# x, B, C and twelve gate blocks as seven block products at the front, staged in DRAM, with the state-space chunks beside the heads

## Chip, core and metric

The kernel runs on one core of a Trainium2 chip. The metric is device time in microseconds (us) for one launch, on that core. TensorE (PE) multiplies, VectorE (DVE), ScalarE (ACT) and GpSimd (POOL) do the elementwise work, and SyncE (SP) issues nearly all DMAs, in one queue and in the order of the program.

## What is computed

One decoder layer with two causal token mixers side by side, 1024 tokens by 1024 channels, all in float32:

```
h = RMSNorm(x)
[q|k|v|z_a | xBC | z_s | dt | gates] = h @ w_in        # 4096 + 3072 + 2048 + 32 + 2048 columns
attention: 8 heads, two softmax maps each, a = p0 - lam*p1, RMS-normed, times silu(z_a)  -> y_a
state space: xBC = silu(conv4(xBC)); 32 heads in 4 groups, 8 chunks of 128 tokens a group;
             group RMSNorm(y * silu(z_s))                                                -> y_s
merged = sigmoid(g_a)*(y_a @ w_proj_attn) + sigmoid(g_s)*(y_s @ w_proj_ssd)
out = x + merged @ w_out
```

Float32 products are kept accurate by splitting each operand into a high and a low part in the fp32r format: high·high + high·low + low·high, three matmuls for each product. The split is a ScalarE copy (high) and a subtraction on VectorE or GpSimd (low).

## The kernel before

The normalised h lies transposed in SBUF as two tiles, hH and hL (8 row blocks of 128 channels by 1024 tokens). Four kinds of projection run over it, all in matmuls of 512 output columns, and this order is the bulk of TensorE's program (`bulk`): head 0, dt, heads 1 to 7 (`att_proj`, PSUM tile pma), z of group 0 (pmz), then per group x, B and C (`ssd_proj_xbc`, pc) and z, then sixteen gate blocks (`gates`, pg). An attention head's scores, softmax, transposes and value product (`att_core`, `att_block`: sc, p, pa, av, pya) run beside the projections of the following heads. A group's eight chunks (`ssd_core`, `ssd_chunk`: px, pb, pO, pS, pD, py, and the decay tile ab) run beside the projections of the next group, and the last group's beside the gates. x, B and C go through a depthwise convolution of four taps (`conv`: three VectorE passes of nearly 1024 columns, then tanh on ScalarE and one more pass) and stay in SBUF as tiles cv, as z stays in tiles zs.

At the end come three products (`products(c)`: the two halves of y_s, then y_a, against their weights) and the output projection (`final`, po). These three products already go by a scheme with seven block multiplications for a 2 x 2 by 2 x 2 block product, where the plain one has eight. Its sums of the left operand, t1 to t4, are made on GpSimd and staged in DRAM (`prepare`, `sums_of`, t_d), read back and split into forms (`fill`), its sums of weights are made in `pair_splits`, and its seven products go into three PSUM banks X, Y and Z that are recombined in `pair_step`:

```
ORDER = (("b11", 1), ("t2", 6), ("b21", 2), ("t3", 7), ("t1", 5), ("t4", 4), ("b22", 3))
BEFORE = {2: "ct", 7: ("u", 6), 4: ("u", 7), 3: "c22"}
into = {1: x, 6: y, 2: x, 7: y, 5: z, 4: y, 3: z}
```

BEFORE names what must have been read out of a bank before the product of that number may go into it.

The order of every engine's program is fixed when the kernel is built, by a planner in the kernel itself (`Plan`). Each stage is a generator that emits instructions and yields the time at which it wants to go on. Costs are formulas in the helpers; on VectorE an op of n columns is put down as 0.07 + 0.00104 n us (`tt`, `stt`), whatever it meets on the chip. The bulk generator runs whenever no task is due. Buffers are counted in Slots: 19 large SBUF tiles (bigs), 12 of 2 KB a partition (mids), 4 raw weight tiles, 9 split weight tiles, and PSUM in three rings: mm 2 banks, sc 2 tiles of 2 banks, tr 2 banks. `PACE` is the planned time between chunk starts, 13 us. On the chip the engines keep that order and wait on semaphores.

In the profile most instructions carry a helper's line: L167 is every matmul, L176 every transpose, L191 every ScalarE activation, L196 two-tensor ops of VectorE and GpSimd, L201 VectorE's scalar-tensor-tensor ops, L213 every DMA, L647 the masked score copy. So the groups are told apart by tile names.

## Time and profile before

| | |
|---|---|
| median of 3 runs | 1678.44 us (1678.04 to 1679.87) |
| profiled execution | 1677.29 us, span 1675.5 us, granted clock 0.998 |
| TensorE, VectorE, ScalarE, GpSimd busy | 1638.2, 1084.8, 815.9, 530.5 us |
| matmul records | 8226 |
| DMA | 194.47 MB, mean 116 GB/s |
| heads (first matmul to last) | 11.0 to 563.8 us |
| x, B, C (pc) | 626.2 to 1065.7 us |
| gates (pg) | 1122.5 to 1338.3 us |
| three products | 1338.5 to 1583 us |

A row of a group reads: line, engine, operation, what it writes <- reads, shape, xcount | total busy us, mean ns of one | idle time of the engine before them and what ended it. A row of a table by stage reads: stretch, its length, then for each engine busy us and instruction count, then TensorE's granted clock, the DMA engines' busy share and GB/s. A row of waits reads: who waited for whom, total us, times, longest us.

### The profile page before, as it was taken

What the parts mean: (1) busy time and instruction counts of PE and PEld (TensorE: products, weight loads), DVE (VectorE), ACT (ScalarE), POOL (GpSimd) and SP (SyncE); (2) the same over time, 40 slices, a digit from 0 to 9 for tenths busy, and PEclk for the clock granted to TensorE, in tenths of its full rate; (3) what the DMA queues carried; (4) which work ended last, traced back from release to release, by engine and by line L of the source; (5) the groups of instructions that cost most, each with busy time, mean ns of one, the idle gap of its engine ahead of it and who ended that gap; (6) DMA issues with size and microseconds to landing.
All of it is one profiled execution on the core that took longest, in us unless ns stands there. A gap on an engine that the chain in (4) does not pass through costs nothing.

```text
span 1675.5 us, 23517 instructions
## 1 busy us (share of the span) xinstructions
PE 1638.2 (98%) x8226; PEld 1364.6 (81%) x8226; DVE 1084.8 (65%) x1902; ACT 815.9 (49%) x1971; POOL 530.5 (32%) x616
## 2 busy tenths in 40 slices
PE   7999999999999999999999999999999999989999
PEld 5788888888888888888888888888778887767887
DVE  6686676666765744589578658846654167878821
ACT  5646566565665542466365455535534245233410
POOL 4323233231341210132243233236764433333100
PEclk9999999999999999999999999999999999999999
DMA  6202021120210202322142133227769657787832
GB/s 191 55 19 64 7 58 34 31 63 7 57 51 14 63 29 69 87 88 64 50 133 83 39 101 107 57 81 245 257 214 334 211 167 264 238 289 244 290 120 69
DMA packets 168740, 194.47 MB, mean 116 GB/s; under 512 B 11557, under 2 KB 114734, under 8 KB 168622
## 3 DMA queue, kind: packets, MB, share of 16 engines
q1 hardware_dynamic: 168622, 192.97, 35.9%
q8 instruction: 65, 1.06, 0.3%
q14 instruction: 53, 0.43, 0.1%
HBM read 143.51 MB, written 49.41 MB: 115 GB/s over the span
## 4 chain that ended last, share of the span: by engine, by line
PE 82%; DVE 5%; POOL 4%; issue 4%; ACT 3%; DMA 2%; SPq 0%; POOLq 0%; DVEq 0%; ACTq 0%
PE pma L167 17%; PE pc L167 15%; PE pmz L167 9%; PE pg L167 7%; PE po L167 5%; PE pY L167 4%; PE sc L167 4%; PE av L167 4%; PE pX L167 3%; PE pD L167 3%; PE pZ L167 2%; PE pa L176 2%; POOL ts L196 1%; ACT qh L191 1%; PE pS L167 1%
## 5 line engine op out<-in xcount | busy, mean ns | idle before, releaser
L167 PE MATMUL pma<-w,hH 128*128 128x512 f32 x1024 | 343.0, 405 | 0.1
L167 PE MATMUL pc<-hH,w 128*128 128x512 f32 x768 | 243.5, 394 | 0.0
L167 PEld LDWEIGHTS pma<-w,hH 128*128 128x128 f32 x1024 | 189.2, 190 | 34.6 <-ACT hH L191 0.5
L167 PE MATMUL pma<-w,hL 128*128 128x512 f32 x512 | 206.4, 403 | 0.0
L191 ACT ACTIVATE w<-raw 128x512 fp32r<-128x512 f32 (+1 forms) x194 | 120.4, 625 | 126.8 <-PE pc L167 45.7
L196 POOL TENSOR_TENSOR w<-raw,w 128x512 fp32r<-128x512 f32 (+1 forms) x62 | 83.2, 1342 | 265.1 <-ACT w L191 259.2
L167 PEld LDWEIGHTS pc<-hH,w 128*128 128x128 f32 x768 | 142.9, 188 | 28.1
L167 PE MATMUL pmz<-w,hH 128*128 128x512 f32 x512 | 165.4, 397 | 0.0
L167 PE MATMUL pg<-hH,w 128*128 128x512 f32 x512 | 161.9, 393 | 0.0
L196 DVE TENSOR_TENSOR w<-raw,w 128x512 fp32r<-128x512 f32 x132 | 111.1, 848 | 66.5 <-ACT w L191 65.1
L167 PE MATMUL pc<-hL,w 128*128 128x512 f32 x384 | 151.6, 395 | 0.0
L191 ACT ACTIVATE p<-p,nm 128x256 f32<-128x256 f32 (+7 forms) x128 | 98.2, 769 | 46.2 <-DVE nm L647 46.2
L167 PEld LDWEIGHTS pg<-hH,w 128*128 128x128 f32 x512 | 95.8, 188 | 19.3
L167 PEld LDWEIGHTS pma<-w,hL 128*128 128x128 f32 x512 | 97.0, 189 | 16.9 <-DVE hL L196 0.3
L167 PEld LDWEIGHTS pmz<-w,hH 128*128 128x128 f32 x512 | 94.8, 188 | 18.3
L191 ACT ACTIVATE wp<-rawp 128x512 fp32r<-128x512 f32 x72 | 45.4, 631 | 125.9 <-PE pY L167 37.5
L167 PE MATMUL pmz<-w,hL 128*128 128x512 f32 x256 | 100.9, 394 | 0.0
L167 PE MATMUL pg<-hL,w 128*128 128x512 f32 x256 | 100.8, 394 | 0.0
L201 DVE SCALAR_TENSOR_TENSOR cv<-pc,cols,cv 128x1023 f32<-128x1023 f32 (+2 forms) x72 | 91.8, 1275 | 12.0 <-ACT cv L191 11.5
L647 DVE CUSTOM_DVE_ANT_0 p<-sc,maskb 128x256 f32<-128x256 f32 (+7 forms) x128 | 91.5, 752 | 12.2 <-PE sc L167 11.6
L191 ACT ACTIVATE ab<-ab,nac 128x128 f32<-128x128 f32 x256 | 77.9, 389 | 27.6 <-POOL ab L934 27.6
L223 POOL TENSOR_TENSOR f<-ssv,e 128x1 f32<-128x1 f32 x64 | 13.7, 214 | 245.1 <-ACT av L191 224.9
(267 smaller groups left out, 3544.4 us busy)
## 6 DMA issues: line engine op xcount, KB each, us to landing
raw<-in_w_in_dram SPq DMA_DIRECT2D x176, 256.0 KB, 3.2
ab<-act_d SPq DMA_DIRECT2D x32, 512.0 KB, 5.3
t_d<-ts SPq DMA_DIRECT2D x24, 512.0 KB, 2.9
ys_d<-xdt SPq DMA_DIRECT2D x32, 256.0 KB, 2.5
gt_d<-gt SPq DMA_DIRECT2D x32, 256.0 KB, 4.7
ts<-ys_d SPq DMA_DIRECT2D x16, 512.0 KB, 6.5
rawp<-in_w_proj_ssd_dram SPq DMA_DIRECT2D x16, 512.0 KB, 5.9
gl<-gt_d SPq DMA_DIRECT2D x32, 256.0 KB, 4.9
```

The lines of the kernel that those rows point to most:

```text
L167: nc.tensor.matmul(o, lhsT=lhsT, rhs=rhs, start=start, stop=stop, **kw)
L176: nc.tensor.transpose(out=o, in_=i, identity=ident if idn is None else idn)
L191: nc.scalar.activation(o, i, f, **kw)
L196: (nc.vector if eng == "V" else nc.gpsimd).tensor_tensor(out=o, in0=a, in1=b, op=op)
L201: nc.vector.scalar_tensor_tensor(out=o, in0=a, scalar=s, in1=b, op0=op0, op1=op1)
L223: nc.gpsimd.tensor_tensor(out=dst, in0=src, in1=add, op=ALU.add)
L647: nc.vector.tensor_tensor_reduce(out=p[:, 0:n], in0=sc[:, 0:n], in1=maskb[:, S - n:S], scale=-1.0, scalar=3e38, op0=ALU.add, op1=ALU.min, ...
```

## The change

The combined projection is reordered and most of x, B, C and the gates go by the scheme of seven products.

- *Order* (`ORDER1`): z 0, dt, z 1, then pairs of 128-column blocks: twelve of x/B/C ("c") and, after every second one, a pair of gate blocks ("g"), with z 2 and z 3 among them; then the eight heads; then the four gate blocks that are left; then products and output as before.
- *`front_pair`*: seven products of 4 x 3 matmuls into three banks. The left operand's forms t1 to t4 are made in SBUF from h by `form_evac` (tokens 512 to 1023 against 0 to 511, channels in two halves) and fill 16 of the 17 large tiles while the front lasts. `conv_step` recombines and convolves each half of 512 tokens by itself, with three short ops at the seam; `gate_step` recombines and takes tanh.
- *Staging*: convolved x, B, C go to DRAM (cv_d), z too (z_d); a chunk loads its x, B, C and z again.
- *Chunks* start one by one through all groups (`ssd_all`) from when their group's blocks are in DRAM: one each 60 us (`SLOW`) while the front holds the large tiles, one each 20 us (`PACE`) from the heads on. One decay tile ab instead of a share of all large ones, and a chunk's ab multiplication is placed after its state update.
- *PSUM*: the rings tr and sc become one ring of six banks. Scores of more than 512 keys take two banks, each reduced by itself, with a minimum of two columns after it.
- *Buffers*: 17 large, 16 of 2 KB; shares (`Share`) cap what each stage may hold. Weight pairs load as four tiles of 512-byte rows instead of two of 1 KB rows.
- *End*: sums for the products are made as soon as their groups and heads are done; reading forms (`fill`) is started before the last four gate blocks.

The diff, cut to its core:

```diff
 C_ZS = 7168
 C_DT = 9216
 C_GATE = 9248
-NBIG, NW, NRAW, NMID, NSM = 19, 9, 4, 12, 8
-PACE = 13.0
+NBIG, NW, NRAW, NMID, NSM = 17, 9, 4, 16, 8
+PACE = 20
+FRONT, SLOW = 12, 60.0
 WPOOL = 3
...
     ps_mm = ctx.enter_context(tc.tile_pool(name="ps_mm", bufs=2, space=bass.MemoryType.PSUM))
-    ps_sc = ctx.enter_context(tc.tile_pool(name="ps_sc", bufs=2, space=bass.MemoryType.PSUM))
-    ps_tr = ctx.enter_context(tc.tile_pool(name="ps_tr", bufs=2, space=bass.MemoryType.PSUM))
+    ps_tr = ctx.enter_context(tc.tile_pool(name="ps_tr", bufs=6, space=bass.MemoryType.PSUM))
...
+    cv_d = dram.tile([3072, S], F32, name="cv_d")
+    z_d = dram.tile([GROUPS, S, 512], F32, name="z_d")
...
+    trs, mms, qlos = Slots(6), Slots(2), Slots(2)
+    trs.line = []
     ws, raws = Slots(NW), Slots(NRAW)
+    qkm, atm, ytm, smids = Share(mids, 4), Share(mids, 4), Share(mids, 2), Share(mids, 10)
+    heads, abb = Share(bigs, 8), Share(bigs, 1)
...
+    CONV = (16, 20, 0, 2, 4, 6, 18, 22, 8, 10, 12, 14)
+    ORDER1 = [("z", 0), ("dt", 0), ("z", 1)]
+    for i in range(12):
+        ORDER1 += [("c", CONV[i])] + ([("g", i - 1)] if i % 2 else [])
+        if i in (5, 9):
+            ORDER1.append(("z", 2 if i == 5 else 3))
+    FPAIRS = [i for i in ORDER1 if i[0] in "cg"]
+    ORDER1 += [("setup", 0)] + [("h", h) for h in range(HEADS)]
+
...
+                ks = yield from pl.get(raws, 4)
+                raw = [rpool.tile([P, 4, P], F32, tag="raw", name=f"rawf{i}{q}") for q in range(4)]
+                raw_of[i] = (raw, ks, [load(raw[q], wlist[i][q // 2][:, :, q % 2 * P:(q % 2 + 1) * P]) for q in (0, 1, 2, 3)])
...
+        t3 = tt(b22, b22, b12, ALU.subtract, pl.t)
+        yield max(t11, t3)
+        t1 = tt(b12, b12, r11, ALU.subtract, max(t11, t3))
+        t2 = tt(r11, b22, r11, ALU.add, t1)
+        yield t2
+        t4 = tt(r21, r21, r11, ALU.subtract, max(t2, t21), "G")
+        t2 = yield from split("t2", r11, t2)
+        t3 = yield from split("t3", b22, t3)
+        mids.give(k22, t3)
+        t1 = yield from split("t1", b12, t1)
+        mids.give(k12, t1)
+        mids.give(ks[0], max(t2, t4))
+        t4 = yield from split("t4", r21, t4)
...
+            nms, t1 = [], at
+            for i, j in enumerate(range(0, n, 512)):
+                e = min(n, j + 512)
+                nms.append(tin(1, "nm"))
+                nc.vector.tensor_tensor_reduce(out=p[:, j:e], in0=sc[i][:, 0:e - j], in1=maskb[:, S - n + j:S - n + e],
+                                               scale=-1.0, scalar=3e38, op0=ALU.add, op1=ALU.min, accum_out=nms[i])
+                t1 = pl.op("V", 0.08 + 1.042e-3 * (e - j), t1 - HOP if i else t1)
+                trs.give(k[i], t1)
+            nm = nms[-1]
+            if len(nms) > 1:
+                t1 = tt(nm, nms[0], nm, ALU.min, t1 - HOP)
...
+    def front_pair(kind, b, last):
+        ids = w_next(7)
+        ks = []
+        for q in (trs, mms, trs):
+            ks.append((yield from pl.get(q, first=True)))
+        x, y, z = trt(f"fX{kind}{b}"), mmt(f"fY{kind}{b}"), trt(f"fZ{kind}{b}")
+        into = {1: x, 6: y, 2: x, 7: y, 5: z, 4: y, 3: z}
+        cell = {"kc": (yield from pl.get(mids)), "x": x, "ks": ks}
+        step = conv_step if kind == "c" else gate_step
+        for n, (f, p) in enumerate(ORDER):
+            while p in BEFORE and (BEFORE[p] not in cell and (p != 3 or kind == "c" or ("c22g" not in cell))):
+                yield pl.t + 0.1
+            yield from w_need(ids[n])
+            if f[0] == "t":
+                while any(("formed", t) not in ready for t in range(4, NT)):
+                    yield pl.t + 0.2
+                at = max(ready["formed", t] for t in range(4, NT))
+                if at > pl.t:
+                    yield at
+            wt = wts[ids[n]]
+            for i in range(4):
+                yield from steps3(into[p], (wt[:, 0, i, :], wt[:, 1, i, :]), front_form(f, i),
+                                  i == 0 and p in (1, 6, 5), i == 3, skip_group_check=True)
+            if last and f[0] == "t":
+                for part in range(2):
+                    for kp in range(2):
+                        bigs.give(forms_t[f, part, kp][1], pl.t + 0.1)
+            w_done(ids[n])
+            pl.spawn(step(b, p, into[p], cell), pe_done())
...
+    def conv_step(b, p, ps, cell):
+        at = pe_done()
+        kx, ky, kz = cell["ks"]
+        if p in (1, 6, 7):
+            yield from front_sum(p, ps, cell, at)
+        elif p == 2:
+            yield from conv(b, 0, ps, cell, at)
+        elif p == 4:
+            k = cell["kc"]
+            at = tt(ps, cell["c"], ps, ALU.add, max(at, cell["u", 7][2]))
+            mids.give(k, at)
+            yield from conv(b + 1, 0, ps, cell, at, (mms, ky))
+        elif p == 5:
+            while ("u", 7) not in cell or ("conv", b, 0) not in cell:
+                yield pl.t + 0.1
+            u, k, t = cell["u", 7]
+            x = cell["x"]
+            cell["c22"] = at = tt(x, u, ps, ALU.add, max(at, t, cell["conv", b, 0]))
+            mids.give(k, at)
+            yield from conv(b + 1, 1, x, cell, at, (trs, kx))
+        else:
+            u, k, t = cell["u", 6]
+            at = tt(ps, u, ps, ALU.add, max(at, t))
+            mids.give(k, at)
+            yield from conv(b, 1, ps, cell, at, (trs, kz))
+
+    def conv(b, h, ps, cell, at, free=None):
+        km = yield from pl.get(mids)
+        cv = midt(name=f"cv{h}")
+        yield max(at, pl.t)
+        if h == 0:
+            tail = tin(3, "tail")
+            cell["tail", b] = (tail, act(tail, ps[:, 509:512], AF.Copy, at))
+        at = act(cv, ps, AF.Identity, at, bias=cbc(b), scale=cwc(3, b))
         for j in (1, 2, 3):
             yield at
-            at = stt(cv[:, j:S], pm[:, 0:S - j], cwc(3 - j, b), cv[:, j:S], ALU.mult, ALU.add, at)
...
+        at = load(cv_d[b * P:(b + 1) * P, h * 512:h * 512 + 512], cv, at)
+        mids.give(km, at)
+        cv_at[b, h] = at
...
+        at = load(z_d[g, t * P:(t + 1) * P, :], zz, at)
+        mids.give(km, at)
+        z_at[g, t] = at
...
-            while c - state["n"] >= 2:
+            while c - state["n"] >= 2 or c and c - 1 not in state["did"]:
                 yield pl.t + 0.2
             pl.spawn(ssd_chunk(g, c, state, abs_))
-            yield pl.t + PACE
+            yield pl.t + (PACE if bigs.avail(3) <= pl.t or 'setup' in ready else SLOW)
...
+        kxr = yield from pl.get(smids)
+        xr = midt([P, 4, P], name=f"xr{g}{c}")
+        at = load(xr, cv_d[g * 512:(g + 1) * 512, cs].rearrange("(b p) t -> p b t", p=P))
+        kbc = yield from pl.get(sms, 2)
+        bT, cT = smt(f"bT{g}{c}"), smt(f"cT{g}{c}")
+        t_bc = load(bT, cv_d[(16 + g) * P:(17 + g) * P, cs])
...
+        zc = midt(name=f"zc{g}{c}")
+        t_z = load(zc, z_d[g, cs, :])
+        yield max(t_m, t_dt, pl.t)
...
+        for c, g in ((0, 1), (1, 3)):
+            while ready.get("ssd", {}).get(g, INF) > pl.t:
+                yield pl.t + 0.5
+            yield from sums_of(c, range(4))
+            if c == 0:
+                pl.spawn(prepare_a())
+
+    def prepare_a():
         for i in range(4):
-            ready["summing"] = 1
+            while len([t for t in ready.get("att", []) if t <= pl.t]) < 10 + 2 * i:
+                yield pl.t + 0.5
...
+    def ssd_all():
+        for g in range(GROUPS):
+            while "tables" not in ready:
+                yield pl.t + 0.5
+            yield from ssd_core(g)
+
     def bulk():
-        yield from att_proj(0)
-        yield from dt_proj()
-        for h in range(1, HEADS):
-            yield from att_proj(h)
-        yield from ssd_proj_z(0)
-        yield from ssd_proj_xbc(0)
-        pl.spawn(ssd_core(0))
-        for g in range(1, GROUPS):
-            yield from ssd_proj_xbc(g)
-            yield from ssd_proj_z(g)
-            pl.spawn(ssd_core(g))
+        pl.spawn(ssd_all())
+        pl.spawn(prepare())
+        step = {"z": ssd_proj_z, "h": att_proj}
+        for kind, i in ORDER1:
+            if kind in "cg":
+                yield from front_pair(kind, i, (kind, i) == FPAIRS[-1])
+            elif kind in step:
+                yield from step[kind](i)
+            else:
+                yield from dt_proj() if kind == "dt" else att_setup()
+        pl.spawn(fill())
         yield from gates()
         lag[:] = [0.0135, 2.5]
         for c in range(3):
             yield from products(c)
         yield from final()
```

More of the change, by code (lines that the diff above doesn't have):

```diff
@@ L56, in give, with __init__, avail, take @@
         self.free[k] = at
+class Share:
+    def __init__(self, ring, n):
+        self.ring, self.own = ring, Slots(n)
+    def avail(self, n=1):
+        return max(self.ring.avail(n), self.own.avail(n))
+    def take(self):
+        return self.own.take(), self.ring.take()
+    def give(self, k, at):
+        self.own.give(k[0], at)
+        self.ring.give(k[1], at)
 class Plan:
@@ L541, in tile_hybrid_layer, with att_setup @@
     lefts = {}
+    def att_setup():
+        ready['setup'] = 1
+        for i in range(2):
+            kqlo.append((yield from pl.get(bigs)))
+            q = bigt([P, 2, 512], F32R, name=f"qlo{i}")
+            nc.gpsimd.memset(q[64:P, 0].bitcast(F32), 0.0)
+            nc.gpsimd.memset(q[0:64, 1].bitcast(F32), 0.0)
+            qlo.append(q)
     def att_proj(h):
@@ L1092, in ssd_chunk @@
         state["n"] += 1
-        if last:
-            for i in gx[g]:
-                bigs.give(i[1], pl.t)
         yield at
-        k = yield from pl.get(trs)
+        k = yield from pl.get(trs, first=True)
         py = trt(f"py{g}{c}")
@@ L1115, in gates @@
     def gates():
-        for ob in range(16):
+        for ob in range(FRONT, 16):
             ids = w_next(2)
@@ L1446, in bulk @@
         yield from final()
[L1448 to L1449 removed]
+    kn = [mids.take() for _ in range(2)]
+    nwb = [midt(name=f"nwb{i}") for i in range(2)]
     def start():
         load_x(0)
[L1453 removed]
+        for i in range(2):
+            load(nwb[i], norm_w[:, i * 512:i * 512 + 512].partition_broadcast(P).rearrange("p a d -> p (a d)"))
         yield from w_loads(0, 4)
```

450 lines of the change are left out of this document (259 added, 191 removed).

## Prediction

> **What bounds the kernel now.** I read the page first (shares, chain), then a table of busy time by stage, then the waits of TensorE, then the groups of VectorE by shape.
>
> ```profile
> span 1675.5 us, 23517 instructions
> PE 1638.2 (98%) x8226; PEld 1364.6 (81%) x8226; DVE 1084.8 (65%) x1902; ACT 815.9 (49%) x1971; POOL 530.5 (32%) x616
> PE 82%; DVE 5%; POOL 4%; issue 4%; ACT 3%; DMA 2%; SPq 0%; POOLq 0%; DVEq 0%; ACTq 0%
> ```
>
> TensorE is busy for 98% of the span and carries 82% of the chain, so a matmul less is worth its pace, and time lost elsewhere counts only where TensorE waits for it. The stages, cut where the first matmul of each begins (start to head 0, heads 1 to 7, z 0 with the last head's core, x/B/C/z with chunks, gates with the last chunks, gates alone, the three products):
>
> ```profile
> core 0: us, PE busy (x) PEld busy (x) DVE busy (x) ACT busy (x) POOL busy (x), PEclk, DMA share, GB/s
> 0.00:75.40 75.40, 62.82 (x315) 50.49 (x316) 48.47 (x110) 45.17 (x116) 28.43 (x52) 1.00 0.39 113
> 75.40:555.60 480.20, 476.77 (x2600) 399.90 (x2599) 326.20 (x827) 284.63 (x817) 142.57 (x235) 1.00 0.14 40
> 626.00:1122.00 496.00, 495.52 (x2499) 416.44 (x2498) 351.33 (x447) 245.91 (x540) 134.35 (x144) 1.00 0.26 77
> 1122.00:1240.00 118.00, 112.63 (x591) 93.33 (x591) 79.74 (x103) 63.49 (x162) 82.26 (x71) 1.00 0.73 240
> 1240.00:1338.00 98.00, 98.00 (x437) 81.21 (x437) 27.61 (x32) 30.48 (x54) 45.59 (x36) 1.00 0.77 268
> 1338.00:1416.00 78.00, 78.00 (x346) 64.61 (x345) 49.57 (x69) 39.46 (x71) 29.02 (x20) 1.00 0.61 203
> 1416.00:1498.00 82.00, 72.09 (x311) 58.07 (x310) 69.14 (x98) 30.27 (x53) 28.42 (x20) 0.99 0.80 271
> ```
>
> TensorE idles 12.6 us at the start, 3.4 us in seven heads, 0.5 us in 496 us of x/B/C/z, 9.9 us when the second product takes over from the first. VectorE is at 68% in the heads (326.2 / 480.2), 71% beside x/B/C (351.3 / 496), 28% in the gates alone. What TensorE waits for:
>
> ```profile
> PE ph L176 <- DVE x L201: 10.6, 3, 8.9
> PE pY L167 <- DVE u L196: 8.2, 4, 6.0
> PE pO L167 <- DVE cl L196: 5.1, 5, 2.2
> ```
>
> The total is small because matmul records overlap, but it names the engine: where TensorE waits, it waits for VectorE.
>
> **The change part by part.**
>
> *Matmuls removed.* A pair of 128-column blocks now costs 2 blocks x 2 halves x 8 rows of weights x 3 passes = 96 matmuls of 512 columns. As seven products it costs 7 x 4 x 3 = 84. There are 12 pairs of x/B/C and 6 pairs of gates, so 18 x 12 = 216 go. Their pace, from a window that holds nothing but gates:
>
> ```profile
> 1250.00:1330.00 80.00, 80.00 (x355) 66.26 (x354) 8.84 (x15) 1.00 0.72 260
> ```
>
> 80 / 355 = 0.225 us each, so 216 x 0.225 = **-48.7 us**, all on the bounding engine. The Trainium skill ("TensorE: Matmul & The Clock Gate", section "Wait — 56ns, not 53.3ns?") gives 215.7 ns for such a matmul; by that the saving would be 46.6 us. The window decides.
>
> *The front (z 0, dt, z 1, twelve conv pairs, six gate pairs, z 2, z 3).* What a conv pair costs VectorE, by rows of the same kinds of instruction:
>
> ```profile
> L201 DVE SCALAR_TENSOR_TENSOR cv<-pc,cols,cv 128x1023 f32<-128x1023 f32 x24 | 30.7, 1279 | 11.5 <-ACT cv L191 11.5
> L201 DVE SCALAR_TENSOR_TENSOR zs<-zs,pmz 128x512 f32<-128x512 f32 x32 | 21.9, 685 | 46.5 <-ACT zs L191 46.5
> L196 DVE TENSOR_TENSOR u<-pc,pY 128x512 f32<-128x512 f32 x24 | 16.4, 685 | 13.9 <-PE pY L167 13.3 <-ACT hH L191 0.6
> L196 DVE TENSOR_TENSOR wp<-rawp,wp 128x512 fp32r<-128x512 f32 x60 | 46.0, 770 | 49.7 <-ACT wp L191 48.6 <-DMA acc_d<-u 0.8
> ```
>
> The convolution's four 1.28 us passes per block become eight of 0.685: 16 x 0.685 = 11.0 us a pair. The recombining adds are 5 x 0.685 = 3.4, six weight splits 6 x 0.77 = 4.6 (a pair needs seven weight tiles where it needed four), six short ops at the halves' seam about 1.2 (an estimate at a quarter of a 512-column op each). That is 20.2 us of VectorE for 84 x 0.225 = 18.9 us of TensorE. A gate pair has the adds and splits alone, 8.0 us. Two conv pairs and a gate pair: 48.4 of 56.7 us, 85%. With one state-space chunk (8.5 us, below) each 60 us, 93% or so; z 2 and z 3 (43 us of TensorE, some 10 of VectorE each) thin it out. The chain that can stop TensorE inside a pair is: product 2 into bank X, convolution of that bank, then the fifth sum written into X, before product 3 may use bank Z again. The products stage has the same chain today:
>
> ```profile
> 1421.42 3.01 PE L167 MATMUL pX<-f1b,wp 128*128 128x512 f32 x12 [1.11 <-ACT pc L191]
> 1425.20 3.01 PE L167 MATMUL pY<-f1t,wp 128*128 128x512 f32 x12 [0.76 <-DVE u L196]
> 1432.12 0.98 PE L167 MATMUL pY<-hL,wp 128*128 128x512 f32 x3 [1.19 <-DVE u L196]
> 1436.01 0.93 PE L167 MATMUL pZ<-hL,wp 128*128 128x512 f32 x3 [0.83 <-DVE pX L196]
> ```
>
> With VectorE crowded this pair loses 1.11 + 0.76 + 1.19 + 0.83 = 3.9 us. In the first product (1338 to 1416, VectorE 49.6 of 78 us) none is lost. So a conv pair costs 0 to 3.9 us, 0 to 47 us in twelve. I take 1 us each, **+12 us**: the average of 85 to 93% is nearer to the crowded pair, but z and gate pairs let the queue drain every second or third pair. A wait in VectorE's queue there delays u, the splits and the bank's release alike, and the next product stands behind them.
>
> *Forming t1 to t4 of h* for four token blocks is about 3 adds and 8 splits of VectorE, three adds of GpSimd and 8 copies of ScalarE each, some 6 us of VectorE a block. Cover: z 0, dt and z 1, 94 us of TensorE in which VectorE has mostly splits; needed at the first conv pair. Cost nothing; without the cover up to 6 us. The start keeps its wait for x (10.6 us): weights and x are split as before.
>
> *Heads beside chunks.* The front ends near 11 + 4 x 43 + 7 + 18 x 18.9 = 530 us, plus chunks. Group 0 is whole after four conv pairs, about 220 us in; at one chunk each 60 us some five run in the front and 27 remain for the heads, at one each 20 us. VectorE per chunk: thirteen groups, first and last
>
> ```profile
> L196 DVE TENSOR_TENSOR ab<-ab,cb 128x1024 f32<-128x1024 f32 x32 | 44.3, 1384 | 13.3 <-ACT ab L191 11.8 <-ACT cb L191 1.4
> L196 DVE TENSOR_TENSOR bl<-pb,bh 128x128 fp32r<-128x128 f32 x28 | 8.0, 285 | 8.7 <-ACT bh L191 8.6
> L196 DVE TENSOR_TENSOR cl<-cv,ch 128x128 fp32r<-128x128 f32 x28 | 18.3, 654 | 0.0
> ```
>
> sum to 271 us over 32 chunks, 8.5 each. TensorE per chunk, from one chunk's rows:
>
> ```profile
> 865.76 1.97 PE L167 MATMUL pD<-xdt,ab 128*128 128x64 f32 x16
> 868.32 0.60 PE L176 MATMUL px<-ident,cv 128*128 128x128 f32 x4
> 860.39 0.39 PE L167 MATMUL pO<-sh,cl 128*128 128x512 f32 x1
> ```
>
> about 1.8 + 2 x 0.45 + 6 x 0.225 + 0.3 = 4.3 us. A head is 480.2 / 7 = 68.6 us with 326.2 / 7 = 46.6 us of VectorE, plus 1.5 (estimate) for scores taken in pieces of 512. So 20 us hold one chunk (4.3 of TensorE) and 15.7 / 68.6 = 0.23 of a head: VectorE 8.5 + 0.23 x 48.1 = 19.5, **98%**. ScalarE: 284.6 / 480.2 = 59% x 0.79 plus about 6 us a chunk (190 us over 32), 77%. What does TensorE lose at 98%? The nearest rows are two windows beside x/B/C where VectorE is at 84%:
>
> ```profile
> 700.00:800.00 100.00, 99.93 (x522) 84.15 (x521) 84.39 (x109) 61.66 (x145) 34.71 (x38) 1.00 0.25 78
> 1000.00:1100.00 100.00, 99.65 (x526) 84.21 (x526) 84.12 (x112) 54.38 (x127) 30.02 (x34) 1.00 0.24 69
> ```
>
> They lose nothing: the lower bound is 0. For the upper: the scheduler lays VectorE out at 0.07 + 0.00104 x 512 = 0.604 us an op where the rows say 0.685, 13% more; if every planned busy stretch ends with TensorE waiting, it loses 13% of the stage's VectorE work, 0.13 x (8 x 48.1 + 27 x 8.5) = 80 us. I take a sixth, **+13 us**: the 84% rows stand at zero, but nothing today shows 98%.
>
> ```profile
> L934 POOL TENSOR_SCALAR_AFFINE_SELECT ab<-ab 128x1024 f32<-128x1024 f32 x32 | 38.2, 1196 | 8.3 <-DMA ab<-act_d 8.1
> L196 POOL TENSOR_TENSOR xn<-xn,dsk 128x512 f32<-128x512 f32 x32 | 38.4, 1200 | 2.5
> ```
>
> GpSimd rises in the heads: about 4.4 us a chunk (two rows above at 1.2, a second product at 1.1, 0.9 for the root) and 142.6 / 7 = 20.4 a head, so 4.4 + 0.23 x 20.4 = 9.1 of 20 us, 46% where it has 30% now. The row cl above takes 654 ns and bl, the same size out of PSUM, 285: both operands of cl lie in SBUF. The Trainium skill ("SBUF — State Buffer", section "SBUF: two separate sides") says why this would speak against the change: a VectorE op with two SBUF inputs and a GpSimd op that reads SBUF take the shared port pair in turn, and the loser blocks for the whole instruction. By that rule some 320 such ops would meet a GpSimd op 16 points more often, about 0.6 us each time, 31 us of VectorE on top, and the sum would end near 1685. The rows' averages hold some of it already, so the sum leaves it out.
>
> *Chunks' own waits.* xr, bT, cT and z now come by DMA, and each chunk holds one ab tile; its chain grows by landings:
>
> ```profile
> raw<-in_w_in_dram SPq DMA_DIRECT2D x176, 256.0 KB, 3.2
> ab<-act_d SPq DMA_DIRECT2D x32, 512.0 KB, 5.3
> ```
>
> Staging adds 80 stores and 128 loads, and products' weights 24 loads, on SP's one queue, where a store waits for its data and holds the loads behind it (weights, and the chunk's xr, for which TensorE's next transposes wait). 42 MB more move, in stages where DMA is at 10 to 26%. Cost nothing: chunks have until the second product, some 120 us after the heads (43 of gates, 78 of the first product), and weights run nine tiles ahead. If a chunk takes 25 us, 27 x 25 = 675 us still ends with the heads.
>
> *Gates and products.* Only four gate blocks, 4 x 48 x 0.225 = 43 us, stand between heads and products instead of 216, to load the first forms. Sums of groups 0/1 and of heads 0 to 6 are done in the heads by then. Cost nothing; if the forms come late, the price is like the handover at 1416 to 1438, 8 to 25 us. It could also gain up to 5 us, the sums for the second product being done early. One ring of six banks replaces 2 + 4: more freedom for scores, no cost.
>
> Sum: 1675.5 - 48.7 + 12 + 13 = 1651.8 us of span. The profiled execution took 1677.3 us, 1.8 above its span, and the median of the runs is 1678.4, so the sum is 24 us under: **1654 us**.
>
> **Rivals.** (a) *All covers hold*: 1678.4 - 48.7 = 1630. For it: VectorE at 84% costs nothing today. Against: 98%. (b) *VectorE becomes the bound in the heads*, slower than before: its 614 us of work there stand against 549 + 27 x 4.3 = 665 us of TensorE, so it decides once the loss passes 49 us, 8% of that work; at the full 13% it is 1630 + 80 = 1710. For it: the same 13% of underestimate, GpSimd at 46%; against: the 84% windows. A long wait costs twice:
>
> ```profile
> 1496.70 1.65 PE L167 MATMUL pY<-hL,wp 128*128 128x512 f32 x3 [6.01 <-DVE u L196]
> ```
>
> after 6 us of waiting three matmuls take 1.65 us, against 0.98 us after the wait of 1.19 above. (c) *The conv chain stops TensorE in every pair* as at 1421: 1630 + 47 + 13 = 1690, slower; against: the gate pairs between. (d) *Forms late at the products*: 1654 + 25 = 1679, no change; against: the sums' loads and adds move into the heads, where DMA is at 14%.
>
> **Numbers.** Likeliest 0.46, with its own range 1640 to 1672; (a) 0.24, (b) 0.16, (c) 0.07, (d) 0.07. A measurement of this kernel can tell some 0.2%, 3.4 us. Faster: 0.46 + 0.24 and half of (d), 0.74. Same: 0.06. Slower: (b), (c) and the edge of (d), 0.20. The range leaves out (b) and reaches from (a) to (c): 1628 to 1692.
>
> **What would show it.** Right: 8010 matmul records; TensorE's busy time near 1590; in the front VectorE at 85 to 93% with waits of about 1 us on the pair's third product; in the heads VectorE at 95% or more and TensorE's idle time 2 to 3%, its waits named after VectorE. Wrong: VectorE under 90% in the heads (a), TensorE idle over 8% there (b), chunks still running when the second product starts, or long waits for DMA.

## The result and the profile after

The changed kernel is slower: 1748.72 us, the median of four runs (1746.12 to 1751.27), against 1678.97 us. The ratio is 1.0415 (95% interval 1.0396 to 1.0434), 70 us, where the prediction had 24 us the other way. The profiled execution spans 1749.6 us at a mean granted clock of 0.976; before, 1675.5 us at 0.998. The page after:

```profile
span 1749.6 us, 24401 instructions
...
PE 1640.4 (94%) x8010; PEld 1346.3 (77%) x8010; DVE 1275.1 (73%) x2463; ACT 877.1 (50%) x2155; POOL 636.2 (36%) x694
...
PE 55%; DVE 24%; ACT 8%; issue 5%; DMA 4%; POOL 3%; SPq 0%; DVEq 0%; POOLq 0%; ACTq 0%
```

The 216 matmuls are gone (8226 to 8010), yet TensorE is busy as long as before, 1640.4 against 1638.2 us: the other matmuls became longer, in large part because the granted clock was lower (below). Its share of the chain fell from 82% to 55%, VectorE's rose from 5% to 24%. By stage, cut where the first matmul of each begins (start; front pairs with z 2 and z 3; heads with chunks; last gates; three products; output):

```profile
core 0: us, PE busy (x) PEld busy (x) DVE busy (x) ACT busy (x) POOL busy (x), PEclk, DMA share, GB/s
0.00:128.30 128.30, 111.25 (x503) 86.62 (x504) 87.69 (x148) 57.24 (x121) 35.40 (x45) 0.99 0.34 113
128.30:625.10 496.80, 472.33 (x2092) 385.81 (x2091) 348.62 (x563) 218.80 (x430) 155.21 (x129) 0.98 0.37 115
625.10:1328.10 703.00, 662.95 (x3689) 556.44 (x3688) 569.84 (x1355) 452.67 (x1331) 322.69 (x427) 0.98 0.35 107
1328.10:1396.30 68.20, 62.37 (x316) 51.86 (x315) 44.59 (x91) 34.70 (x74) 24.25 (x25) 0.97 0.50 161
1396.30:1658.90 262.60, 243.92 (x1010) 192.38 (x1009) 201.54 (x273) 105.40 (x186) 94.53 (x67) 0.96 0.77 256
1658.90:1749.60 90.70, 87.62 (x409) 73.19 (x407) 22.79 (x35) 8.24 (x13) 4.17 (x3) 1.00 0.37 123
```

What a stage lost is measured against its matmuls at full pace, by the prediction's own rows. Front: (18 x 84 + 384) x 0.225 + 6 chunks x 4.3 = 452 us, so 45 are lost. Heads: 8 x 68.6 + 26 x 4.3 = 661, so 42. The products took 245.0 us before, so 18 more. The start is 10 us longer than with no forms in the front (e4, below), and TensorE idles 5.8 us in the gates (68.20 less 62.37). 1626.8 (the old span less the matmuls) + 45 + 42 + 18 + 10 + 6 = 1748, for a span of 1749.6. These floors are estimates, good to some 5 us.

The waits name VectorE for the most part, as predicted (19 of 24 us in the front, 29 of 40 in the heads), but the largest two are of two kinds:

```profile
PE pa L201 <- DVE p L226: 12.9, 14, 3.7
...
PE fZc L192 <- DVE fXc L221: 10.5, 6, 3.0
```

`fZc <- fXc` is the seven products' chain: product 3 may use bank Z only when the fifth sum stands in bank X. `pa <- p` is the heads' softmax. First the chain, VectorE's instructions by start and length (us):

```profile
480.32 0.21 DVE L226 SCALAR_TENSOR_TENSOR cv<-tail,cols,cv 128x3 f32<-128x3 f32 x1
480.46 1.52 DVE L226 SCALAR_TENSOR_TENSOR cv<-fXc,cols,cv 128x510 f32<-128x510 f32 x2
481.89 0.68 DVE L226 SCALAR_TENSOR_TENSOR cv<-fZc,cv 128x512 f32<-128x512 f32 x1
482.71 0.69 DVE L226 SCALAR_TENSOR_TENSOR cv<-fXc,cv 128x512 f32<-128x512 f32 x1
483.31 0.69 DVE L221 TENSOR_TENSOR fYc<-fc,fYc 128x512 f32<-128x512 f32 x1
483.91 0.69 DVE L221 TENSOR_TENSOR fXc<-fu,fZc 128x512 f32<-128x512 f32 x1
484.51 0.68 DVE L221 TENSOR_TENSOR w<-raw,w 128x512 fp32r<-128x512 f32 x1
```

VectorE works almost without a gap, convolution passes, then two sums; `fXc` is written at 484.6. No record here is longer than its shape usually is, and GpSimd ran a single op in this time (480.46 to 481.76): VectorE simply has this much to do first. TensorE has had nothing to do for 2.28 us by then, and pays again afterwards:

```profile
484.65 0.50 PE L192 MATMUL fZc<-hH,wp 128*128 128x512 f32 x1 [2.28 <-DVE fXc L221]
484.99 0.46 PE L192 MATMUL fZc<-hL,wp 128*128 128x512 f32 x1
485.25 1.05 PE L192 MATMUL fZc<-hH,wp 128*128 128x512 f32 x2
...
489.54 0.62 PE L192 MATMUL fXg<-hH,wp 128*128 128x512 f32 x2
```

```profile
484.60:489.00 4.40, 4.35 (x12) 3.46 (x13) 1.91 (x3) 0.95 (x2) 0.00 (x0) 0.61 0.58 188
489.00:495.00 6.00, 6.00 (x29) 4.95 (x28) 5.71 (x9) 3.30 (x6) 1.30 (x1) 1.00 0.19 49
```

Two matmuls take 1.05 us after the wait and 0.62 from 489.5 on; the granted clock of the stretch is 0.61, then 1.00. A mean clock of 0.976 over 1749.6 us is 42 us of lost clock in all, against 1675.5 x 0.002 = 3.4 before. By stage it is 12 us in the front, 17 in the heads and 10 in the products; these are part of the losses above.

In the heads VectorE itself is held up. VectorE, then GpSimd, in the same microseconds:

```profile
1131.06 0.81 DVE L226 SCALAR_TENSOR_TENSOR cc<-s,cols,rec 128x1 f32<-128x1 f32 x1
1131.79 0.15 DVE L226 SCALAR_TENSOR_TENSOR e<-s 128x1 f32<-128x1 f32 x1
1131.90 1.35 DVE L226 SCALAR_TENSOR_TENSOR p<-p,cc 128x256 f32<-128x256 f32 x1
1133.18 1.48 DVE L221 TENSOR_TENSOR qk<-qk,rs 128x256 f32<-128x256 f32 x1
...
1134.77 1.03 DVE L226 SCALAR_TENSOR_TENSOR cc<-s,cols,rec 128x1 f32<-128x1 f32 x1
...
1135.83 1.58 DVE L226 SCALAR_TENSOR_TENSOR p<-p,cc 128x384 f32<-128x384 f32 x1
```

```profile
1130.56 1.30 POOL L221 TENSOR_TENSOR xdt<-xn,dtt 128x512 f32<-128x512 f32 x1 [1.93 <-ACT xn L216]
1131.93 1.04 POOL L221 TENSOR_TENSOR xn<-xn,dsk 128x512 f32<-128x512 f32 x1
1132.93 1.45 POOL L221 TENSOR_TENSOR ts<-ts,ts 128x512 f32<-128x512 f32 x1
1134.46 1.32 POOL L221 TENSOR_TENSOR ts<-ts 128x512 f32<-128x512 f32 x1
1135.74 1.26 POOL L221 TENSOR_TENSOR w<-raw,w 128x512 fp32r<-128x512 f32 x1
```

All but the shortest of these VectorE ops (`e`) end within 0.4 us after one of GpSimd's ends, as if the two took turns. One column (`cc`) takes 0.81 and 1.03 us. TensorE waited 3.72 us for `p` behind this and then ran at a clock of 0.57 for 4 us. By tile, the lengths in ns (shortest/median/longest):

```profile
L226 DVE SCALAR_TENSOR_TENSOR cc<-s,cols,rec x64: 219/220/1130, 665.7 to 1378.2; 128x1 f32<-128x1 f32 x64
```

```profile
L226 DVE SCALAR_TENSOR_TENSOR y<-y,f,zg x64: 334/351/1373, 675.8 to 1387.9; 128x128 f32<-128x128 f32 x64
```

```profile
L221 DVE TENSOR_TENSOR u<-pc,pY x24: 672/686/689, 1404.6 to 1652.1; 128x512 f32<-128x512 f32 x24
```

`cc` and `y`, with all inputs in SBUF, stretch to 1.1 and 1.4 us; `u`, which reads a bank of PSUM, never passes 689 ns. Summed over all VectorE records that last over 0.2 us longer than their shape usually does, this is 129 us in 160 ops after, 72 us in 100 ops before. GpSimd ends an op inside every one of these records after. The text calls this sum *blocking* from here on; 54 us of it lie in the heads and 24 in the front.

In the products the longest waits are for the reading forms, which lie in `hH` and `hL` by then:

```profile
PE pZ L192 <- DVE hL L221: 5.9, 6, 2.9
PE pY L192 <- DVE hH L221: 4.0, 3, 2.2
PE pZ L192 <- DVE hH L221: 2.5, 4, 1.4
```

### The profile page after: what moved, and what is told of

Read it like the earlier page. It is cut to its first block, busy times and chain, and to the rows that moved or that the text cites. A ratio compares the mean times of both kernels' runs of the same rounds, so it can differ in the third digit from the quotient of the medians.

```text
span 1749.6 us, 24401 instructions
## 1 busy us (share of the span) xinstructions
PE 1640.4 (94%) x8010; PEld 1346.3 (77%) x8010; DVE 1275.1 (73%) x2463; ACT 877.1 (50%) x2155; POOL 636.2 (36%) x694
## 3 DMA queue, kind: packets, MB, share of 16 engines
q8 instruction: 63, 1.03, 0.3%
## 4 chain that ended last, share of the span: by engine, by line
PE 55%; DVE 24%; ACT 8%; issue 5%; DMA 4%; POOL 3%; SPq 0%; DVEq 0%; POOLq 0%; ACTq 0%
PE pma L192 9%; PE pmz L192 7%; PE po L192 5%; PE pY L192 4%; DVE cv L226 3%; PE pX L192 3%; PE fYg L192 3%; PE av L192 2%; PE pZ L192 2%; PE fZc L192 2%; DVE p L747 2%; PE pD L192 2%; PE fXc L192 2%; PE fXg L192 2%; PE fZg L192 2%
## 5 line engine op out<-in xcount | busy, mean ns | idle before, releaser
L221 POOL TENSOR_TENSOR rawf<-rawf,rawf 128x512 f32<-128x512 f32 x90 | 124.9, 1388 | 275.6 <-DVE wp L221 147.9
L216 ACT ACTIVATE wp<-rawf 128x512 fp32r<-128x512 f32 x180 | 110.8, 627 | 128.9 <-POOL rawf L221 27.5
L221 DVE TENSOR_TENSOR wp<-rawf,wp 128x512 fp32r<-128x512 f32 x150 | 123.1, 832 | 39.3 <-ACT wp L216 37.3
L216 ACT ACTIVATE w<-raw 128x512 fp32r<-128x512 f32 (+1 forms) x122 | 74.9, 624 | 97.2 <-PE po L192 32.0
L192 PE MATMUL fYc<-ft,wp 128*128 128x512 f32 x432 | 107.5, 396 | 5.3 <-DVE fu L221 5.3
L747 DVE CUSTOM_DVE_ANT_0 p<-sc,maskb 128x512 f32<-128x512 f32 (+2 forms) x192 | 98.6, 551 | 3.7 <-PE sc L192 3.4
L192 PEld LDWEIGHTS fYc<-ft,wp 128*128 128x128 f32 x432 | 81.6, 191 | 24.1 <-DVE fu L221 7.3
L192 PE MATMUL av<-v,at 128*128 128x128 f32 x576 | 76.4, 277 | 1.4 <-DVE at L234 0.7
L192 PEld LDWEIGHTS av<-v,at 128*128 128x128 f32 x576 | 71.9, 192 | 7.2 <-DVE at L234 1.7
L249 POOL TENSOR_TENSOR rs<-rs,mhalf 128x4 f32<-128x4 f32 (+1 forms) x71 | 72.3, 1018 | 5.9
## 6 DMA issues: line engine op xcount, KB each, us to landing
raw<-in_w_in_dram SPq DMA_DIRECT2D x104, 256.0 KB, 3.1
rawf<-in_w_in_dram SPq DMA_DIRECT2D x72, 256.0 KB, 4.0
cv_d<-cv SPq DMA_DIRECT2D x48, 256.0 KB, 2.0
z_d<-zs SPq DMA_DIRECT2D x32, 256.0 KB, 2.0
xr<-cv_d SPq DMA_DIRECT2D x32, 256.0 KB, 3.8
zc<-z_d SPq DMA_DIRECT2D x32, 256.0 KB, 3.2
```

Source lines behind the costliest of these rows:

```text
L192: nc.tensor.matmul(o, lhsT=lhsT, rhs=rhs, start=start, stop=stop, **kw)
L216: nc.scalar.activation(o, i, f, **kw)
L221: (nc.vector if eng == "V" else nc.gpsimd).tensor_tensor(out=o, in0=a, in1=b, op=op)
L249: nc.gpsimd.tensor_tensor(out=dst, in0=dst, in1=mhalf[:, 0:cols], op=ALU.pow)
L747: nc.vector.tensor_tensor_reduce(out=p[:, j:e], in0=sc[i][:, 0:e - j], in1=maskb[:, S - n + j:S - n + e], scale=-1.0, scalar=3e38, op0=ALU ...
```

## The experiments

Two theories: (T1) *blocking*, GpSimd's ops holding VectorE's ("port theory" in the expectations); (T2) *order*, VectorE's hand-over times set by its load and by an order that the planner lays without room, above all the seven products' chain ("load theory"). The stages (us) of every run, cut as above, and the mean clock, all of the profiled execution, which lies within 7 us of its run's median:

| run | ratio to before | start | front | heads | gates | products | clock |
|---|---|---|---|---|---|---|---|
| after | 1.0415 | 128.3 | 496.9 | 702.9 | 68.2 | 262.6 | 0.976 |
| e1 GpSimd's sums cut | 1.0061 | 127.8 | 484.0 | 669.1 | 63.4 | 247.3 | 0.992 |
| e2 planner told of turns | 1.0477 | 121.3 | 519.4 | 676.9 | 57.8 | 286.7 | 0.973 |
| e3 VectorE costed +15% | 1.0178 | 128.0 | 507.2 | 657.3 | 60.6 | 258.5 | 0.985 |
| e4 front as plain halves | 1.0334 | 118.3 | 509.8 | 688.9 | 65.3 | 261.8 | 0.986 |
| e5 front's splits to GpSimd | 1.0071 | 130.0 | 472.8 | 675.1 | 64.7 | 256.0 | 0.993 |
| e6 e5 with e3, pace 18 | 1.0020 | 128.6 | 469.9 | 661.4 | 64.3 | 262.4 | 0.989 |
| e7 extra GpSimd ops, reading | 1.0344 | 130.9 | 497.2 | 699.5 | 66.7 | 253.0 | 0.979 |
| e8 extra GpSimd ops, not reading | 1.0228 | 127.6 | 496.3 | 679.5 | 65.2 | 250.8 | 0.988 |
| e9 e5, +15% in the heads alone | 1.0066 | 128.1 | 472.8 | 673.3 | 63.6 | 261.9 | 0.989 |
| e10 e9, products' splits to GpSimd | 1.0149 | 129.8 | 479.0 | 670.6 | 66.1 | 269.7 | 0.985 |
| e11 e9 with +10% | 1.0036 | 129.3 | 473.2 | 668.5 | 64.2 | 257.2 | 0.992 |
| e12 e6 without room in products, late forms | 1.0012 | 130.7 | 473.9 | 661.9 | 64.5 | 258.4 | 0.989 |
| e13 e12, two gate pairs at the end | 0.9994 | 130.3 | 436.2 | 665.2 | 104.7 | 248.6 | 0.992 |

**e1: GpSimd's in-place sums cut to one column.** The kernel so leaves these sums out (weights' sums, sums of y, xn times dsk). The order stays.

```diff
+        if eng == "G" and cut:
+            f = (lambda v: v[:, :, 0:1]) if len(o.shape) == 3 else (lambda v: v[:, 0:1])
+            nc.gpsimd.tensor_tensor(out=f(o), in0=f(a), in1=f(b), op=op)
...
-        t1 = tt(a21, a21, a22, ALU.add, max(at), "G")
+        t1 = tt(a21, a21, a22, ALU.add, max(at), "G", True)
...
```

> The changed kernel with the same planned order, but GpSimd's in-place sums (weights' sums in pair_splits, the sums of y for the products, the chunk's xn times dsk) work on one column only, so their results are left out: about 230 of 636 us of GpSimd. Port theory (GpSimd ops block VectorE ops whose two inputs lie in SBUF, and TensorE waits for those): a good third of the blocking goes, with its share of half-clock stretches: 1700 to 1720 us. Load theory (VectorE has too much work in too tight an order, blocking is a side matter): 1740 to 1750, since no VectorE op is taken away.

Measured 1690.53 us, 1.0061 (1.0041 to 1.0082). Front and heads:

```profile
127.80:611.80 484.00, 467.41 (x2093) 383.70 (x2092) 328.88 (x562) 218.30 (x430) 92.13 (x129) 0.98 0.38 118
611.80:1280.90 669.10, 647.68 (x3689) 545.24 (x3688) 544.83 (x1355) 452.15 (x1331) 265.88 (x427) 1.00 0.36 112
```

With as many VectorE instructions, these are 25 us shorter in the heads (544.8 for 569.8) and the stage 34; blocking falls from 129 to 52 us. These sums cost 58 us of time by the medians, more than either theory expected. Between the two profiled executions it is 67: 34 in the heads, 13 in the front, 15 in the products. The cut also lets GpSimd's results come earlier, so it does not prove blocking alone; e7 and e8 bear on that.

**e2: the planner lays GpSimd's ops and VectorE's with all inputs in SBUF one after another.**

```diff
-        s = max(self.e[eng], after, self.t)
+        s = max(self.e[eng], after, self.t, self.e["L"] if port else 0.0)
...
```

> The changed kernel with all its work; only the planner is told that a GpSimd op and a VectorE op with two SBUF inputs never run at once. Port theory: the order now leaves room where blocking happens, TensorE's waits shrink: 1700 to 1735 us. Load theory: no better than the general slack of e3, or slower, 1745 to 1765, because the order is laid out longer.

Measured 1758.39 us, 1.0477 (1.0458 to 1.0496): heads 26 us shorter, front 22 and products 24 longer. T1 had 1700 to 1735 here, T2 1745 to 1765. Blocking hardly falls (120 us): planning the turns does not keep the ops apart on the chip. That the order itself is laid out longer would fit the longer front and products; no run isolates it.

**e3: VectorE's costs 15% higher for the planner, no instruction changed.**

```diff
+        cost *= 1.15 if eng == "V" else 1.0
```

> The changed kernel with all its work; the planner puts every VectorE op down 15% longer, without regard to the port. Load theory: this is what the order lacks, 1705 to 1730 us. Port theory: 15% of 0.6 us doesn't cover a block of 1.1 us, so little changes: 1735 to 1755.

Measured 1708.88 us, 1.0178 (1.0162 to 1.0194).

```profile
128.00:635.20 507.20, 471.76 (x2093) 387.17 (x2092) 348.53 (x563) 219.06 (x430) 156.56 (x129) 0.97 0.37 113
635.20:1292.50 657.30, 640.03 (x3689) 545.42 (x3688) 568.81 (x1357) 451.52 (x1331) 324.43 (x424) 1.00 0.36 111
```

The heads lose nothing now, at the same VectorE time (568.8 us, 569.8 without the change) and the same blocking (54 us there in both): in this order, laid with room, the blocked ops do no harm. The front loses 10 us more, and it is the chain:

```profile
PE fZc L193 <- DVE fXc L222: 27.8, 7, 8.2
```

Room in the order does not shorten a chain that TensorE must wait for inside one pair. So the two stages lose for two reasons.

**e4: x, B, C and the twelve gate blocks as plain halves, 96 matmuls a pair, no forms of h in the front.**

```diff
-            wlist.append(pair_w(w_in, 0, (C_XBC if kind == "c" else C_GATE) + i * P))
+            for b in (i, i + 1):
+                wlist += block_w(w_in, KB, (C_XBC if kind == "c" else C_GATE) + b * P)
...
```

> The changed kernel's order, staging, banks and chunk pacing, but x, B, C and the twelve gate blocks by plain products (eight of eight), without the sums of weights, of h and of results. 216 matmuls more, 48.7 us. If the loss comes from reorder and staging alone: 1748 + 49, about 1797 us. If the seven products' side work makes half of the loss: 1750 to 1770. Port theory lies between, since 125 us of GpSimd's weight sums go.

Measured 1735.89 us, 1.0334 (1.0316 to 1.0351).

```profile
0.00:118.30 118.30, 108.73 (x503) 86.22 (x503) 56.86 (x101) 41.78 (x79) 15.16 (x31) 1.00 0.40 129
118.30:628.10 509.80, 509.80 (x2341) 423.77 (x2340) 260.70 (x428) 185.96 (x377) 71.48 (x70) 1.00 0.38 114
```

The plain front never waits and takes 509.8 us; seven products take 496.8, so of 48.7 us there remain 13, and the start gives back 10: the seven products' gain in start and front is 3 us. The heads are 14 us longer with them than without (702.9 for 688.9), and with 216 matmuls fewer the kernel is 13 us slower than e4. The rest of the change, the new order with staging and chunks beside the heads, costs 57 us by itself (1735.89 - 1678.93).

**e5: the six weight splits of a front pair move from VectorE to GpSimd.**

```diff
-        u11 = yield from split(a11, at[0], "V")
+        u11 = yield from split(a11, at[0], E)
...
```

`E` is "G" for the pairs of the front, and all six splits take it.

> The changed kernel with all its work; the low parts of the front's split weights (six of seven in each pair, 108 ops) are made on GpSimd instead of VectorE. GpSimd gets busier (about 636 to 760 us), VectorE loses 65 us and nearly all its two-input SBUF ops in the front. Port theory: blocked time in the front goes although GpSimd works more; TensorE's waits in the front fall by 20 to 35 us with their half-clock stretches, the heads stay: 1710 to 1728. If GpSimd's sheer load decides: front weights come late, 1750 or more.

Measured 1691.89 us, 1.0071 (1.0056 to 1.0086).

```profile
130.00:602.80 472.80, 461.79 (x2092) 377.69 (x2091) 298.89 (x460) 216.14 (x431) 285.03 (x235) 1.00 0.39 119
602.80:1277.90 675.10, 649.36 (x3687) 546.41 (x3687) 572.31 (x1356) 453.77 (x1331) 325.53 (x428) 0.99 0.36 113
```

```profile
PE fZc L192 <- DVE fXc L221: 0.7, 1, 0.7
```

The front gives back 24 of its 45 us and loses no clock; the wait on the chain falls from 10.5 us to 0.7. It does so although GpSimd works there almost twice as long (285 us for 155) and blocking is no less (30 us for 24). In the later runs that keep this edit and all six gate pairs in the front (e6, e9 to e12) the front takes 470 to 479 us, whatever their order. So VectorE's load and its chain decide in the front (63% busy for 70%), T2; blocking has a smaller part at most, the 13 us of e1. The heads' 28 us came without any edit to their instructions, by another order.

**e6: e5 with e3, chunks at a pace of 18.**

> e5, and the planner puts VectorE ops down 15% longer (as in e3), chunks planned each 18 us. Both theories together (blocking in the front taken away, slack in the heads for the rest): 1665 to 1695 us. If e3's gain came from the front alone, nothing adds to e5: 1705 to 1720.

Measured 1681.9 us, 1.0020 (1.0006 to 1.0033): both repairs hold together, one in the front (469.9 us) and one in the heads (661.4); the products stay at 262.

**e7 and e8: four more GpSimd ops a head's token block, which nothing waits for, at one planned cost; in e7 they read SBUF, in e8 they only write it.**

```diff
+        for _ in range(4):
+            nc.gpsimd.tensor_tensor(out=junk[:, 0:P], in0=ident, in1=ident, op=ALU.mult)   # e7
+            nc.gpsimd.memset(junk, 0.0)                                                    # e8
+            pl.op("G", 0.32, t2)
```

> The changed kernel with 256 more GpSimd ops in the heads stage (four after each token block's root), each 128 columns of ident times ident into a scrap tile, about 0.32 us: two inputs read from SBUF. Port theory: VectorE is blocked more, 8 to 25 us slower than the changed kernel (1756 to 1775) and slower than e8. Load theory: same as e8.

> As e7, with the same planned order, but each added GpSimd op is a memset of 256 columns of the scrap tile, about 0.31 us: nothing is read. Port theory: VectorE is not blocked by them; 1745 to 1757, clearly under e7. Load theory: GpSimd's queue is as late as in e7, same time as e7.

Measured 1737.82 us, 1.0344 (1.0323 to 1.0364), and 1717.02 us, 1.0228 (1.0210 to 1.0245). The planned order is the same, so 20.8 us between the two come from the extra ops' kind. Those of e7 and of e8:

```profile
L681 POOL TENSOR_TENSOR junk<-ident x256: 393/401/1910, 636.9 to 1334.3; 128x128 f32<-128x128 f32 x128
```

```profile
L681 POOL MEMSET junk<- x256: 306/312/316, 632.7 to 1308.6; 128x256 f32 x128
```

Those that read are held up to 1.9 us, the five longest behind VectorE ops with all inputs in SBUF; those that only write never, within 10 ns. The blocking goes both ways, and it is about reading SBUF. The Trainium skill ("SBUF — State Buffer", section "SBUF: two separate sides") says that a VectorE op with two SBUF inputs and a GpSimd op that reads SBUF lock each other out for a whole instruction; these rows, `cc` and `u` agree. Not all of the 20.8 us is VectorE being held: the ops that read also keep GpSimd 38 us longer (118 us for 80), and in the heads TensorE waits 5 us more for VectorE and 5 us more for GpSimd itself than in e8. That both runs beat the changed kernel was not expected. One reading, which no run isolates, is that the ops that the planner had to place pushed its order apart, room once more.

**e9, e10, e11: where the room must be.** e9 is e5 with VectorE's cost +15% from the heads to the end of the gates; e11 the same with 10%; e10 is e9 with the products' splits s3, a21 and a22 on GpSimd.

```diff
...
+                if kind == "setup":
+                    pl.slack = 1.15
...
+        pl.slack = 1.0
```

> e5 (front's low parts on GpSimd), and VectorE put down 15% longer by the planner only from the heads to the last gates. If the loss is split by stage (front: VectorE's load; heads: no room for late VectorE), the front takes e5's 473 us, the heads e3's 657 to 661, products about 256: 1665 to 1678 us. If slack in the heads only pushes the waits on into the products: 1680 to 1690.

> e9, and three of the six low parts in each weight pair of the products (s3, a21, a22) on GpSimd too. Load theory for the products: VectorE at 82% is thinned, the stage falls from about 256 to 245 to 250 us, 1655 to 1670. Port theory for the products: GpSimd's longer ops block the form splits more (both their inputs lie in SBUF), no gain or a loss of up to 10 us against e9.

> e9 with 10% in place of 15%. If the room needed in the heads is that of VectorE's late ops (some 56 us of blocking in 571 us of VectorE work, 10%), it does as well as e9 within 5 us; if more is needed, the heads take 665 to 672 and the whole 5 to 10 us more than e9.

Measured 1689.57 us, 1.0066 (1.0052 to 1.0079); 1703.08, 1.0149 (1.0130 to 1.0168); 1684.6, 1.0036 (1.0024 to 1.0048). e9 misses: the heads go from 675.1 to 673.3, not to 660, and 10% does better than 15%. e10 brings no gain either: VectorE's busy share in the products falls (70%, 77% in e9) and they get longer (269.7 us), so a lighter VectorE alone doesn't help them.

**e12: e6 (so with its pace of 18) without the added 15% in the products, and the forms of h for the front begun later.**

```diff
-        yield max(sums12[t, 0][2], sums12[t, 1][2])
+        yield max(sums12[t, 0][2], sums12[t, 1][2], 50 + 10 * (t - 4))
```

> e6, with the forms t1 to t4 of h made later (planned from 50 us, one token block each 10 us) and no added slack in the products. If the forms' VectorE and GpSimd work beside z 0 delays z's evacuation, the start falls from 128 us to about 120: 1668 to 1676 in all. If the start is bound by x and weights alone: 1678 to 1684, as e6.

Measured 1681.31 us, 1.0012 (0.9999 to 1.0025). The heads keep e6's time (661.9), the start isn't shorter (130.7): begun later, the forms cost the start as much.

**e13: e12 with two gate pairs taken out of the front and done plainly between heads and products.** 24 matmuls come back, 5.4 us.

```diff
-FRONT, SLOW = 12, 60.0
+FRONT, SLOW = 8, 60.0
...
-        ORDER1 += [("c", CONV[i])] + ([("g", i - 1)] if i % 2 else [])
+        ORDER1 += [("c", CONV[i])] + ([("g", i - 1)] if i % 2 and i - 1 < FRONT else [])
```

> e12, with two more gate pairs left for the end as plain blocks (eight blocks there instead of four; 24 matmuls more, 5.4 us). If late forms are what the products lose (their cover is 43 us of gates), the products fall from about 256 to 245 to 248 us: 1664 to 1674, even with or under e12. If the products lose to the form splits' blocking itself, nothing comes back: 5 us over e12.

Measured 1677.48 us, the median of eleven runs, against 1679.35: 0.9994 (0.9983 to 1.0004). Gates and products:

```profile
1231.70:1336.40 104.70, 104.14 (x508) 86.73 (x507) 50.82 (x102) 46.72 (x96) 42.00 (x38) 1.00 0.61 204
1336.40:1585.00 248.60, 236.65 (x1009) 191.84 (x1008) 186.18 (x267) 101.16 (x180) 77.28 (x55) 0.98 0.74 246
```

and the products of the kernel before:

```profile
1338.50:1583.50 245.00, 233.57 (x1008) 190.28 (x1008) 188.32 (x267) 102.55 (x179) 77.72 (x55) 0.99 0.73 245
```

With 104.7 us of gates behind which forms can be loaded and made, TensorE idles 0.6 us there, and the products come to within 4 us of what they took before. The whole came out 3.5 us above the range expected. This is the best version found; it cannot be told from the kernel before, and none beats it.

## Why the prediction was wrong, step by step

- **Matmuls removed, -48.7 us: right in size.** 8010 records; the front's floor falls by it. It was all spent again.
- **The front, taken at 12 us of 0 to 47: 45.** The step that failed is the choice of 1 us a pair out of 0 to 3.9, with its reason that "z and gate pairs let the queue drain every second or third pair". In the trace the pairs wait for VectorE all the same, up to 3.0 us at a time, though VectorE was busy 70% of the stage and not 85 to 93%. e4 bounds the gain (13 us in the front, 3 with the start), e5 shows VectorE's work to be the cause: with the splits moved the loss falls to 21 us. Rival (c), given 0.07, named the chain rightly, but that 45 lies next to its 47 is in part chance: the chain stopped TensorE at product 3 six times in twelve pairs, its waits are 16 us (fZc 10.5, fYc 5.3), chunks' waits 8, and 12 us are lost clock, which (c) does not hold.
- **The heads, taken at 13 us of 0 to 80: 42.** The size was nearest to rival (b), but its mechanism was wrong. The 13% "underestimate" came from setting the planner's 0.604 us against a record of 0.685. The conv fence above shows records of 0.69 us whose starts are 0.60 apart: the planner's number is the pace, and a record overlaps the next. The Trainium skill ("Perfetto Trace Analysis", section "Optimizing Scalar/DVE Operations") says as much, that the write's acknowledgement in a record overlaps the next instruction. VectorE's work, put at 614 us, was 569.8, 81% of the stage; the lengths of the records there sum to 650. What stood in its place: VectorE's ops late by about a microsecond behind GpSimd's (e1, and the rows of e7 and e8), in an order without room (e3), and the clock after waits (17 of the 42 us).
- **The shared port, weighed and left out of the sum.** The prediction gave 31 us of VectorE in the heads for it. Over the whole kernel blocking rose by 57 us (72 to 129), and cutting GpSimd's sums was worth 58 us of time. But the heads' 54 us are little more than the same work had before (13 in seven heads, 31 in 626 to 1240 us, where the chunks ran): "The rows' averages hold some of it already" was right in amount there. It failed in the price, since the same amount costs nothing in e3's order and much in this one.
- **The lost clock, in no term.** The prediction says "A long wait costs twice" and gives it no price. It was 42 us, inside the losses of the stages, and most of what TensorE's busy time has over the forecast (1640 us, not 1590).
- **Forms, taken at nothing: about 10 us of start.** The start is 128.3 us with them and 118.3 without (e4). TensorE idles 17 us there, 9.6 in e4; 4.4 of that are waits for VectorE to finish a block of z (zs), which e4 does not have. e12 began the forms later and still waits 5.0 us for zs. What holds VectorE there stays open.
- **Products, taken at nothing: 18.** Rival (d)'s price, 8 to 25 us, and its place were right: TensorE's longest waits there, shown above, are for the reading forms. The cover named for them (four gate blocks, 43 us) looks too short: with more gates there (e13) the loss is 4. One run does not settle it, since with the same four blocks the products took 251 us (e8) to 262 and more in other orders.
- **Gates, taken at nothing: 6** (TensorE's idle time there).
- **Chunks' waits and SP's queue, taken at nothing.** In the heads' waits above 1 us the engines named are VectorE, ScalarE and GpSimd; no DMA price was needed.
- **The signs.** That VectorE under 90% in the heads would mean rival (a) was itself wrong: 81% came with 42 us lost there. A share of busy time says nothing about when an op on the chain ends. TensorE's idle time there, forecast at 2 to 3%, was 5.7%, between the two signs given, with the clock's loss on top.

Together the front missed by 33 us, the heads by 29, the products by 18, the start by 10 and the gates by 6: about the 95 us between 1654 and 1748.72.

**Open.** That room is what the heads lacked rests on many orders, not on one comparison: all seven with 10 or 15% more for VectorE in the heads (e3, e6, e9 to e13) take 657 to 673 us there, and those without it (after, e4, e5, e7, e8) 675 to 703. But why room in the heads alone (e9, e11) brings 2 to 7 us over e5, where room in front and heads (e6, e12) brings 13 to 14, is not known. It may be the pace: e6, e12 and e13 start a chunk each 18 us and not each 20, and no run parts the two. And e5's order without room comes close to e9's with it. The 10 us of the start are open too.

## What to carry to other kernels

A matmul removed from the bounding engine is worth its pace only while the engines that feed it can still deliver on time; when the saving is bought with a longer chain on one of them, price that chain at the one place where the profile shows it crowded, times the number of pairs, and not at the stage's average load (here 47 us for a loss of 45, though in part by chance). In an order that is fixed ahead, give the engine that is held up by chance some room: 15% on VectorE's planned costs, which changes nothing but the order, brought 40 us here, though 10 to 15% on top of e5 brought only 2 to 10. Read an engine's pace from the starts of neighbouring records, not from their lengths.

## What the hardware showed that was not expected

- A wait of 2.28 us inside a busy stretch is followed by 3.4 us at half clock (0.61 over 4.4 us at 484.6; 0.57 over 4 us after 3.72 us at 1137). Eighteen such stretches, each 3.4, 6.8 or 10.2 us long, make the 42 us of lost clock; the kernel before had one. Sixteen of them begin within 3 us of a wait of over 1.5 us. That is no threshold: waits of 1.7 to 2.6 us at 63, 157, 1336 and 1352 us were followed by none, and in the 12 us before the stretch at 1417 us no wait was over 0.9. At 484.6 the stop cost 2.28 us of waiting and (1 - 0.61) x 4.4 = 1.7 us of clock.
- A VectorE op on a single column, 220 ns long, stood up to 1130 ns behind a GpSimd op, and a 401 ns GpSimd op up to 1910 behind VectorE's; a GpSimd memset (312 ns) never passed 316.
